# One-core decoder trunk: V projected together with the forget gate, a reworked recurrent stage, other unit orders and buffer counts

## Chip, core and metric

The kernel runs on one core of one Trainium2 chip. The metric is device time in microseconds (us). It is written in a tile framework: the order of TensorE's instructions is the order of the program text (a manual schedule), the other engines' orders are set by the framework's scheduler, and the framework places all semaphores.

## What is computed

A sequence of 256 tokens with 1024 channels passes through two layers. Layer 0 is FFN, RG-LRU recurrent block, FFN; layer 1 is FFN, forgetting attention, FFN. Keys, values and the forget gate's running sum are computed once, between the layers. Every sub-layer has an RMSNorm before and behind it.

```python
def swiglu(x, w_gate, w_up, w_down):
    return (jax.nn.silu(x @ w_gate) * (x @ w_up)) @ w_down        # 1024 -> 2816 -> 1024

def rg_lru(x, ...):                                               # 16 blocks of 84 channels
    r = sigmoid(blockdiag(x, w_a) + b_a); i = sigmoid(blockdiag(x, w_x) + b_x)
    log_a = -8 * r * softplus(-lam); a = exp(log_a)
    u = sqrt(-expm1(2 * log_a)) * (i * x)
    return scan(h = a * h + u)

def recurrent_block(x, ...):
    gate, rec = split(x @ w_in)                                   # 2 x 1344 columns
    return (gelu(gate) * rg_lru(conv4(rec))) @ w_out

kv = hn @ w_kv; log_f = log_sigmoid(hn @ w_f + b_f); c = cumsum(log_f)   # w_f: 1024 x 16
logits = q k^T + c_q - c_k, causal; softmax; @ v; @ w_o           # 16 heads of 64
```

## The kernel before

**Units.** The 256 tokens are two tiles of 128, t = 0 and t = 1. All weights (float32) stream once through SBUF in units of up to 128 x 1024. A unit is loaded into a `raw` buffer (tag `raw`, `RAW` = 3 of them) by SP's DMA queue, and split (`split`, lines 169 to 182) into a high part `whi` (ScalarE, line 178; the first four units on GpSimd, line 176) and the rest `wlo` (VectorE, line 179). There are `WB` = 10 pairs of these. A product is three matmuls in the reduced float32 format, high by high, high by low, low by high (`mm3`, lines 184 to 188; `mm3w`, 190 to 195, with the weights stationary).

**Order.** `items` is the list of units in the order in which they are loaded, each with a `prep` (load and split) and a `work`. `slot(t, i)` runs the matmuls of unit i for tile t and then calls `tick()`, which counts down the deferred functions (`defer(n, fn)` runs fn n ticks later), prepares the next unit if a pace model says that its load has landed (`prepare_next`, which won't prepare unit i before unit i - WB has been used by both tiles), and takes pieces of VectorE and ScalarE work from `queue`. `run` (line 334) lets tile 0 run ahead of tile 1 by `lag` slots: 7 at the start and end of a stage, 4 (`MID`) in between. So each unit stays in its buffers until tile 1 has used it. One slot is six matmuls of 512 columns.

**FFN stage.** `proj_items` makes the units of the gate and up projections (two blocks of 128 rows by 512 columns each), `row_items` those of the projections back to 1024 channels: there a unit is one block of 128 rows, and each tile accumulates in two PSUM banks. With `rows` = 1 a unit's matmuls run as they come; a higher `rows` holds back the last `rows` units of tile 1 so that all their work for the first bank comes before that for the second. `enter` (line 247) closes such a stage: Squares on ScalarE out of both banks (line 208), the norm's factor on GpSimd (lines 201 and 203), the new `h` on VectorE (line 260), and some ticks later the transposes of `h` (line 217, or with `normed`, used for the first FFN alone, line 284 on a normed copy `hn`) and the split into `xhi` and `xlo`.

**Recurrent stage.** Its order is written out in `RG_ORDER` (line 818). Names such as `0g3` are gate units for tile 0, 11 in three column groups (0 to 3, 4 to 7, 8 to 10); `r2` is a pair of units that gives channels tiles 4 and 5 of the recurrent input for all 256 tokens (`add_rec_units`), followed by the convolution in `conv` (ScalarE line 641, VectorE line 647) and its own split into `ch` (line 649) and `cl` (line 652). `gw2` is a unit of its own with the block-diagonal weights of the two gates, loaded by up to eight small DMAs into a zeroed raw buffer (lines 666 to 676), split like others, and multiplied in three matmuls per product with `ch` and `cl`. Behind it follow tanh (694), scaling on VectorE (711), tanh and exp (714, 715), a Newton step (720 to 725), square root (739), products (744, 745) and the scan (749). For every two pairs, `batch` transposes the gate projection (757), takes its gelu (759), multiplies (771) and splits into `yh` (773) and `yl` (778). w_out (11 row units) follows with `run`; `get_yy` forces the queue's work for group 0, 1 or 2 to be issued before row 0, 4 or 8.

**Shared K/V and attention.** V is two `proj_items` of 512 columns, four units each, with the forget gate's 16 columns as a unit of its own between them (lines 926 to 940); `running` (line 915) makes the running sum nine ticks later. The attention stage has its own order in `ATT_ORDER`: `0` and `1` are slots of tile 0 and 1 for the q and output projections, `a0` and `a1` steps of attention for a tile.

PSUM has four banks `mm`, two `gt`, two `tr`.

Of the kernel before, what the change touches and what calls it, by code (L numbers as in the profile page):

```python
# [28 lines left out]
RAW = 3  # L29
WB = 10  # L30
# [14 lines left out]
def trunk_kernel(ctx: ExitStack, tc: tile.TileContext, A: dict, out: bass.AP):  # L45
# [201 lines left out]
    def enter(t, dests, pf, gb, half, last=False, normed=False):  # L247
# [24 lines left out]
        def norm():  # L272
            stat(t)
            hn = []
            for n in range(2):
                hn.append(hpool.tile([P, 512], F32, tag="t1", name=nm("hn"), bufs=2))
                nc.vector.tensor_scalar(hn[n], h[t][:, n * 512:(n + 1) * 512], rs[t][:, 0:1], None, ALU.mult)

            def go():
                tps = []  # L280
                for n in range(2):
                    tp = gtbank()
                    for j in range(4):
                        nc.tensor.transpose(tp[:, j * P:(j + 1) * P], hn[n][:, j * P:(j + 1) * P], ident)
# [110 lines left out]
    def row_items(w, widths, get_x, post, rows=1):  # L395


        acc = {}
        kept = []
        nk = len(widths)  # L400
        r0 = 0
        for k, kp in enumerate(widths):
            def prep(kp=kp, r0=r0):
                return split(load_raw(w[r0:r0 + kp, :], kp, D), kp, D)

            def work(t, u, k=k):
                if k == 0:
                    acc[t] = [mmbank(), mmbank()]
                if t == 1 and k >= nk - rows:
                    kept.append((k, u))  # L410
                    if k < nk - 1:
                        return
                    todo = [(kk, uu, n) for n in range(2) for (kk, uu) in kept]
# [19 lines left out]
    def ffn_items(pool_of, wg, wu, wd, post_g, next_dests, last=False, normed=False):  # L433
# [55 lines left out]
        row_items(wd, [P] * 22, lambda t, k: (hid[t][0][:, k, :], hid[t][1][:, k, :]), post_down, 4 if last else 1)  # L489
# [46 lines left out]
    sp2 = rw.tile([RT, NRT], F32, name="sp2")  # L536

# [7 lines left out]
    def rg_params():  # L545
# [8 lines left out]
        def rest():  # L554
# [3 lines left out]
            nc.vector.tensor_scalar(sp2, sp, 2.0, None, ALU.mult)  # L558
        defer(1, rest)

# [14 lines left out]
    xcs, chs, tt, th, yy = {}, {}, {}, {}, {}  # L575

    def add_gate_unit(g, k0, kn):
# [5 lines left out]
        def work(t, u):  # L583
# [47 lines left out]
    def conv(p, ps):  # L631
        tl, w = tiles_of(p), pw(p)
        m = len(tl)
# [3 lines left out]
        ch = pools["r"].tile([RT, 2, S], F32R, tag="ch", name=nm("ch"), bufs=2)  # L637
        cl = pools["r"].tile([RT, 2, S], F32R, tag="cl", name=nm("cl"), bufs=2)
        xcs[p], chs[p] = xc, (ch, cl)
# [4 lines left out]
        def taps(j, i):  # L644
# [4 lines left out]
            nc.scalar.activation(ch[:w, j, :], xc[:w, j, :], AF.Copy)  # L649

        def low():
            nc.vector.tensor_tensor(cl[:w, :m, :], xc[:w, :m, :], ch[:w, :m, :].bitcast(F32), ALU.subtract)

        first = [(1.25, ("c", p), lambda j=j, i=i: taps(j, i)) for j, i in enumerate(tl)] + [(0.65, ("c", p), low)]
# [3 lines left out]
    def add_gw_unit(p):  # L658
        tl, w = tiles_of(p), pw(p)
        m = len(tl)  # L660
        n = m * RT if m == 2 else BLK

        def prep():
            raw = new_raw()
            v = raw[:w, :2 * m * n]
# [11 lines left out]
            return split(v, w, 2 * m * n)  # L677

        def work(t, u):
# [3 lines left out]
            ch, cl = chs[p]  # L683
# [16 lines left out]
        rg[f"gw{p}"] = len(items)  # L700
        items.append((prep, work))

    def after_gates(p):
# [3 lines left out]
        t_ = tt[p][:w, :m, :] if p in tt else None  # L707
# [11 lines left out]
        def newton():  # L719
            nc.vector.tensor_scalar(z, z, 0.5, 0.5, ALU.mult, ALU.add)  # L720
            nc.vector.scalar_tensor_tensor(b, tt[p][:w, :m, :], 1.0, z, ALU.add, ALU.mult)
# [6 lines left out]
        queue.extend([(1.1 * s, ("n", p), zz), (1.0 * s, ("n", p), newton), (1.0 * s, ("n", p), newton2)])  # L728
# [3 lines left out]
    def batch(g):  # L732

        pairs = [p for p in (2 * g, 2 * g + 1)]

        def roots():
            for p in pairs:
                v = tt[p][:pw(p), :len(tiles_of(p)), :]
                nc.scalar.activation(v, v, AF.Sqrt)

        def u_of(p):
            w, m = pw(p), len(tiles_of(p))
            v = tt[p][:w, :m, :]
# [3 lines left out]
        def scan(p, j):  # L747
            w = pw(p)
            nc.vector.tensor_tensor_scan(tt[p][:w, j, :], th[p][0][:w, j, :], tt[p][:w, j, :], 0.0, ALU.mult, ALU.add)

        def gelu(t):
            tok = toks[(g, t)]
            tp = trbank()
            y = pools["r"].tile([RT, 4, P], F32, tag="y", name=nm("y"), bufs=2)
# [3 lines left out]
            for (a, b, w) in parts_of(g):  # L758
                nc.scalar.activation(y[:w, a:b, :], tp[:w, a * P:b * P].rearrange("p (a b) -> p a b", a=b - a),
                                     AF.Gelu_apprx_tanh)  # L760
            ys[(g, t)] = y

        def product(t):
            y = ys[(g, t)]
            if t not in yy:
                yy[t] = (pools["r"].tile([RT, NRT, P], F32R, name=f"yh{t}"), pools["r"].tile([RT, NRT, P], F32R, name=f"yl{t}"))
            yh, yl = yy[t]
            for jj, p in enumerate(pairs):
                w, m = pw(p), len(tiles_of(p))
                v = y[:w, 2 * jj:2 * jj + m, :]  # L770
                nc.vector.tensor_tensor(v, v, tt[p][:w, :m, t * P:(t + 1) * P], ALU.mult)
            for (a, b, w) in parts_of(g):
                nc.scalar.activation(yh[:w, 4 * g + a:4 * g + b, :], y[:w, a:b, :], AF.Copy)

        def low(t):
            y, (yh, yl) = ys[(g, t)], yy[t]
            for (a, b, w) in parts_of(g):
                nc.vector.tensor_tensor(yl[:w, 4 * g + a:4 * g + b, :], y[:w, a:b, :],
                                        yh[:w, 4 * g + a:4 * g + b, :].bitcast(F32), ALU.subtract)
# [7 lines left out]
        q.insert(2, (0.0, key, lambda: gelu(0)))  # L787
        q.insert(3, (0.0, key, lambda: gelu(1)))
# [5 lines left out]

    ys = {}
# [7 lines left out]
    add_rec_units(0)  # L803
    add_rec_units(1)
    add_gw_unit(0)
    add_rec_units(2)
    add_gw_unit(1)
    add_rec_units(3)
    add_gw_unit(2)
    for k0 in (0, 3, 6):  # L810
        add_gate_unit(2, k0, min(3, 8 - k0))
    add_rec_units(4)
    add_gw_unit(3)
    add_rec_units(5)
    add_gw_unit(4)
    add_gw_unit(5)
# [11 lines left out]
    def get_yy(t, k):  # L828
        flush(("y", k // 4))
        w = width(k)  # L830
        return yy[t][0][:w, k, :], yy[t][1][:w, k, :]
# [60 lines left out]
    def post_v(n):  # L892
        def f(t, ps):
            nc.scalar.activation(kv["v"][t][:, n * 512:(n + 1) * 512], ps, AF.Copy, scale=rs[t][:, 0:1])
        return f

    def post_f(t, ps):
# [8 lines left out]
        def rest():  # L906
# [5 lines left out]
            defer(9, lambda: running(t))  # L912
# [13 lines left out]
    proj_items(A["w_kv"], D, 512, z_x, post_v(0))  # L926

    def prep_f():
        raw = new_raw()
        nc.sync.dma_start(raw[:, :P].rearrange("p (k n) -> p k n", k=8), A["w_fgate"].rearrange("(k p) n -> p k n", p=P))  # L930
        return split(raw[:, :P], P, P)

    def work_f(t, u):
        ps = mmbank()[:, :NH]
        for k in range(8):
            mm3(ps, *z_x(t, k), u.hi[:, k * NH:(k + 1) * NH], u.lo[:, k * NH:(k + 1) * NH], k == 0, k == 7)
        post_f(t, ps)

    items.append((prep_f, work_f))
    proj_items(A["w_kv"], D + 512, 512, z_x, post_v(1))  # L940
# [92 lines left out]
    for n in range(2):  # L1033
# [11 lines left out]
    ATT_ORDER = ("0 0 0 0 0 0 0 0 a0 1 a0 1 1 a0 1 a0 1 a0 1 a0 1 a0 a1 1 a0 a1 "  # L1045
                 "0 a1 0 a1 0 a1 0 a1 0 a1 0 a1 0 a1 0 a1 1 a1 1 a1 1 1 1 1 1 1")
# [29 lines left out]
    run(n_ffn1, lag_in=3)  # L1076
# [3 lines left out]
    for name in RG_ORDER:  # L1080
# [8 lines left out]
        else:  # L1089
            slot(None, rg[name])  # L1090
    state["a"] = state["b"] = n_rg
    run(n_wout)
# [61 lines left out]
```

## Time and profile before

| | us |
|---|---|
| median of 3 runs (lowest, highest) | 1058.16 (1056.62, 1058.39) |
| the profiled execution | 1056.71 |
| its span, first to last instruction | 1055.0 |
| TensorE busy, weight loads, VectorE, ScalarE | 1019.9, 843.2, 624.0, 539.3 |
| mean granted TensorE clock | 0.982 |
| VectorE's largest group, line 179 (`wlo`), 338 instructions | 408.0 |
| ScalarE's largest group, line 178 (`whi`), 332 instructions | 348.6 |

A page has the busy time of each engine, the span in 40 slices, DMA queues, the chain that ended last and the costliest groups. Matmuls overlap, so their busy time says where TensorE is idle and not how fast it goes; that is read from the starts of successive matmuls. A wait is given as engine, line, what it waited for, then total us, times, and the longest. Windows are stretches of the span with each engine's busy time and the share of the full clock that was granted. Stages by time: first FFN to about 211, recurrent stage to 346, second FFN to 534, K/V and third FFN to about 785, attention to 860, last FFN to the end.

### The profile page before, as it was taken

The numbers are of one execution on the slowest core, as the hardware profiler recorded it, in microseconds if no ns is written. First come the engines' busy times: TensorE is split into PE (matmuls) and PEld (weight loads), VectorE is DVE, ScalarE is ACT, GpSimd is POOL, SyncE is SP. The second block draws the span as 40 slices with busy tenths as digits, with TensorE's granted clock in tenths as the row PEclk, the third lists the DMA queues.
The fourth block names the chain that finished last, engine by engine and source line by source line (L and its number), as shares of the span: only waits on it lengthen the run. The fifth ranks groups of instructions, "written<-read, shape, count | busy, mean of one in ns | idle before, by whom it ended". The sixth has DMA issues, their size and how long they took to land.

```text
span 1055.0 us, 13090 instructions
## 1 busy us (share of the span) xinstructions
PE 1019.9 (97%) x4870; PEld 843.2 (80%) x4870; DVE 624.0 (59%) x771; ACT 539.3 (51%) x739; POOL 48.7 (5%) x109
## 2 busy tenths in 40 slices
PE   7999999989978999999999999999999999999997
PEld 4778888779966888888878888888888888888885
DVE  4666554548997755554486455555476475555542
ACT  3555543538886644443355444444357574454431
POOL 4200000010001100000010000000010010000000
PEclk9999999989988999999999999999999999999999
DMA  5776655536245676655446666655563156766541
GB/s 185 236 221 196 182 188 189 160 88 161 70 158 161 203 213 192 183 181 195 142 160 181 178 180 180 195 182 184 190 203 113 49 161 178 200 180 189 190 140 40
DMA packets 90742, 178.86 MB, mean 170 GB/s; under 512 B 11694, under 2 KB 28150, under 8 KB 90678
## 3 DMA queue, kind: packets, MB, share of 16 engines
q1 hardware_dynamic: 90006, 177.94, 55.9%
q8 instruction: 38, 0.62, 0.2%
q14 instruction: 26, 0.21, 0.1%
q0 software_dynamic: 640, 0.07, 0.1%
q10 hardware_dynamic: 32, 0.01, 0.0%
HBM read 176.95 MB, written 1.05 MB: 169 GB/s over the span
## 4 chain that ended last, share of the span: by engine, by line
PE 83%; DVE 6%; ACT 4%; DMA 4%; issue 2%; POOL 1%; DVEq 0%; SPq 0%; POOLq 0%; ACTq 0%
PE mm L186 25%; PE mm L188 25%; PE mm L187 25%; DVE wlo L179 3%; PE tr L462 2%; DMA raw<-in_ffn_w_gate_dram 2%; ACT whi L178 1%; PE mm L997 1%; PE gt L970 1%; ACT junk L208 1%; DMA raw<-in_ffn_w_up_dram 1%; PE gt L217 1%; PE tr L883 1%; PE mm L195 1%; PE mm L193 1%
## 5 line engine op out<-in xcount | busy, mean ns | idle before, releaser
L179 DVE TENSOR_TENSOR wlo<-raw,whi 128x1024 fp32r<-128x1024 f32 (+3 forms) x338 | 408.0, 1210 | 312.8 <-ACT whi L178 307.6
L178 ACT ACTIVATE whi<-raw 128x1024 fp32r<-128x1024 f32 (+2 forms) x332 | 348.6, 1052 | 359.9 <-PE mm L188 290.9
L186 PE MATMUL mm<-whi,xhi 128*128 128x512 f32 (+2 forms) x784 | 312.3, 398 | 5.3 <-ACT xhi L229 3.3
L187 PE MATMUL mm<-wlo,xhi 128*128 128x512 f32 (+2 forms) x784 | 306.4, 391 | 1.5 <-DVE wlo L179 1.5
L188 PE MATMUL mm<-whi,xlo 128*128 128x512 f32 (+2 forms) x784 | 306.5, 391 | 0.0
L186 PEld LDWEIGHTS mm<-whi,xhi 128*128 128x128 f32 x784 | 148.6, 189 | 35.2 <-POOL whi L176 3.4
L188 PEld LDWEIGHTS mm<-whi,xlo 128*128 128x128 f32 x784 | 148.3, 189 | 31.7 <-DVE xlo L232 0.6
L187 PEld LDWEIGHTS mm<-wlo,xhi 128*128 128x128 f32 x784 | 148.7, 190 | 30.5 <-DVE wlo L179 2.1
L186 PE MATMUL mm<-whi,hhi 128*128 128x512 f32 x352 | 139.5, 396 | 0.0
L188 PE MATMUL mm<-whi,hlo 128*128 128x512 f32 x352 | 139.0, 395 | 0.0
L187 PE MATMUL mm<-wlo,hhi 128*128 128x512 f32 x352 | 138.7, 394 | 0.0
L188 PEld LDWEIGHTS mm<-whi,hlo 128*128 128x128 f32 x352 | 66.1, 188 | 15.4
L187 PEld LDWEIGHTS mm<-wlo,hhi 128*128 128x128 f32 x352 | 66.1, 188 | 15.3
L186 PEld LDWEIGHTS mm<-whi,hhi 128*128 128x128 f32 x352 | 66.1, 188 | 15.1
L456 DVE SCALAR_TENSOR_TENSOR prod<-mm,rstd,sil 128x512 f32<-128x512 f32 (+1 forms) x48 | 33.9, 705 | 37.8 <-PE mm L188 34.0
L447 ACT ACTIVATE sil<-mm,rstd 128x512 f32<-128x512 f32 (+1 forms) x48 | 31.3, 651 | 44.9 <-PE mm L188 44.9
L201 POOL TENSOR_SCALAR nv<-ss 128x1 f32<-128x1 f32 x24 | 9.4, 391 | 759.6 <-ACT junk L208 759.6
L256 DVE TENSOR_TENSOR t<-mm,gb 128x512 f32<-128x512 f32 x24 | 16.3, 688 | 31.1 <-ACT junk L208 30.8
L466 ACT ACTIVATE hhi<-tr 128x512 fp32r<-128x512 f32 (+1 forms) x48 | 26.6, 553 | 14.6 <-PE tr L462 14.5
L467 DVE TENSOR_TENSOR hlo<-tr,hhi 128x512 fp32r<-128x512 f32 (+1 forms) x48 | 30.5, 642 | 3.4 <-ACT hhi L466 1.5
L208 ACT ACTIVATE junk<-mm 128x512 bf16<-128x512 f32 x24 | 14.2, 592 | 33.2 <-PE mm L188 32.8
L186 PE MATMUL mm<-whi,zhi 128*128 128x512 f32 (+1 forms) x80 | 31.0, 387 | 0.0
(178 smaller groups left out, 950.7 us busy)
## 6 DMA issues: line engine op xcount, KB each, us to landing
raw<-in_ffn_w_down_dram SPq DMA_DIRECT2D x88, 512.0 KB
raw<-in_ffn_w_up_dram SPq DMA_DIRECT2D x80, 512.0 KB
raw<-in_ffn_w_gate_dram SPq DMA_DIRECT2D x78, 512.0 KB
raw<-in_rg_w_in_dram SPq DMA_DIRECT2D x20, 504.0 KB
raw<-in_w_kv_dram SPq DMA_DIRECT2D x16, 512.0 KB
raw<-in_ffn_w_gate_dram SPq DMA_DIRECT2D x20, 256.0 KB
raw<-in_rg_w_out_dram SPq DMA_DIRECT2D x10, 504.0 KB
raw<-in_ffn_w_up_dram SPq DMA_DIRECT2D x16, 256.0 KB
```

The lines of the kernel that those rows point to most:

```text
L178: nc.scalar.activation(hi[:parts, c:c + m], rawv[:, c:c + m], AF.Copy)
L179: nc.vector.tensor_tensor(lo[:parts, c:c + m], rawv[:, c:c + m], hi[:parts, c:c + m].bitcast(F32), ALU.subtract)
L186: nc.tensor.matmul(ps, xh, wh, start=first, stop=False)
L187: nc.tensor.matmul(ps, xh, wl, start=False, stop=False)
L188: nc.tensor.matmul(ps, xl, wh, start=False, stop=last)
L208: nc.scalar.activation(junk[:, :src.shape[1]], src, AF.Square, scale=f, accum_out=acc)
L256: nc.vector.tensor_tensor(t1[n], pf[n], gb[:, n * 512:(n + 1) * 512], ALU.mult)
L447: nc.scalar.activation(s[:, :nn], ps, AF.Silu, scale=rs[t][:, 0:1])
L456: nc.vector.scalar_tensor_tensor(pr[:, :nn], ps, rs[t][:, 0:1], s, ALU.mult, ALU.mult)
L462: nc.tensor.transpose(tp[:, j * P:(j + 1) * P], pr[:, j * P:(j + 1) * P], ident)
L466: nc.scalar.activation(hv, tp[:, :nn], AF.Copy)
L467: nc.vector.tensor_tensor(lv, tp[:, :nn], hv.bitcast(F32), ALU.subtract)
```

## The change

- **Buffers.** `RAW` 3 to 5, `WB` 10 to 9.
- **Row units.** `row_items` holds back the last two units by default, for tile 0 as well (tile 0 never more than two); the last FFN keeps four for tile 1.
- **First FFN's end.** `norm` sums the squares of `h` in two halves and is called at once instead of a tick later; its transposes come five ticks on, not two after the one; tile 0 may be 8 slots ahead at the end (`lag_out=8`).
- **Gate projection.** Gelu is taken straight from the PSUM bank in token layout, for (group 0, tile 1) and (group 2, tile 0) only when the next finished one is due, so those banks are held; `batch` transposes the result after the scans, and multiplies out of PSUM.
- **Gates.** No `ch` and `cl`; the block-diagonal weights aren't split and aren't units any more. They are loaded during the first FFN (ahead of its units 20, 26, ... 50) into six buffers of their own and multiplied in plain float32, one matmul instruction per product, with `xc`. `yh` and `yl` later use the same six buffers. `tensor_work`, which feeds the pace model, isn't called for these.
- **After the gates.** Scaling goes into the tanh's and exp's scale and bias (22 ScalarE calls on 256 columns for 12 on up to 512 and 11 VectorE ones); `tt` is one tile for each group of two pairs, so that the square root is one call (two in the last group).
- **Orders.** A new `RG_ORDER`; w_out in a written order `OUT_ORDER`: eight slots of tile 0, four of tile 1, three of 0, seven of 1. A new `ATT_ORDER`.
- **V.** Three column groups of 344, 340 and 340; the first has the 16 forget-gate columns in the same units. Four units each, with `running` fifteen ticks later.

```diff
-RAW = 3
-WB = 10
+RAW = 5
+WB = 9
...
         def norm():
-            stat(t)
+            ss = new_ss()
+            for n in range(2):
+                square_sum(h[t][:, n * 512:(n + 1) * 512], ss[:, n:n + 1])
+            rs[t] = rstd_of(ss, 2)
...
-            defer(2, go)
+            defer(5, go)
...
-            defer(1, norm)
+            norm()
...
-                if t == 1 and k >= nk - rows:
-                    kept.append((k, u))
+                m = rows if t == 1 else min(rows, 2)
+                if k >= nk - m:
+                    kept[t].append((k, u))
...
-                tok = pools["r"].tile([P, 4 * RT], F32, tag="tok", name=nm("tok"), bufs=4)
-                nc.scalar.activation(tok[:, :nn], ps, AF.Copy)
-                toks[(g, t)] = tok
+                if (g, t) not in ((0, 1), (2, 0)):
+                    for gg, tt_ in {(1, 1): [(0, 1)], (2, 1): [(2, 0)]}.get((g, t), []) + [(g, t)]:
+                        n = GCOLS[gg][1]
+                        tok = toks[(gg, tt_)] = pools["r"].tile([P, 4 * RT], F32, tag="tok", name=nm("tok"), bufs=4)
+                        nc.scalar.activation(tok[:, :n], gacc[(gg, tt_)][:, :n], AF.Gelu_apprx_tanh)
...
-            nc.scalar.activation(ch[:w, j, :], xc[:w, j, :], AF.Copy)
-
-        def low():
-            nc.vector.tensor_tensor(cl[:w, :m, :], xc[:w, :m, :], ch[:w, :m, :].bitcast(F32), ALU.subtract)
...
-            raw = new_raw()
-            v = raw[:w, :2 * m * n]
+            v = box["w"] = rw.tile([P, 1024], F32, tag="gy", name=nm("gw"), bufs=6)[:w, :2 * m * n]
...
-            return split(v, w, 2 * m * n)
...
-                        mm3w(ps[:w, j * S:(j + 1) * S], u.hi[:, o:o + w], u.lo[:, o:o + w], ch[:w, k, :], cl[:w, k, :],
-                             k == 0, k == m - 1)
+                        nc.tensor.matmul(ps[:w, j * S:(j + 1) * S], wv[:, o:o + w], xc[:w, k, :],
+                                         start=k == 0, stop=k == m - 1)
...
+        ahead(20 + 6 * p, prep)
+        gw[p] = work
...
-            for j, i in enumerate(tl):
-                nc.vector.tensor_scalar(th[p][0][:w, j, :], th[p][0][:w, j, :], sp2[:w, i:i + 1], sp2[:w, i:i + 1],
-                                        ALU.mult, ALU.add)
-            tt[p] = pools["r"].tile([RT, 2, S], F32, tag="tt", name=nm("tt"), bufs=6)
-            nc.scalar.activation(tt[p][:w, :m, :], z, AF.Tanh)
-            nc.scalar.activation(z, z, AF.Exp, scale=-2.0)
+            for (dst, f, c) in ((t_, AF.Tanh, sp2), (th[p][0], AF.Exp, sp4)):
+                for j, i in enumerate(tl):
+                    nc.scalar.activation(dst[:w, j, :], th[p][0][:w, j, :], f, bias=c[:w, i:i + 1], scale=c[:w, i:i + 1])
...
-        q.insert(2, (0.0, key, lambda: gelu(0)))
-        q.insert(3, (0.0, key, lambda: gelu(1)))
+        q.append((0.0, key, lambda: (gate_T(0), gate_T(1))))
...
-    RG_ORDER = ("0g0 0g1 0g2 0g3 0g4 0g5 0g6 0g7 r0 1g0 1g1 1g2 1g3 r1 gw0 1g4 1g5 r2 gw1 1g6 1g7 r3 gw2 "
-                "0g8 0g9 0g10 r4 gw3 1g8 r5 gw4 1g9 1g10 gw5").split()
+    RG_ORDER = ("0g0 0g1 0g2 0g3 0g4 0g5 0g6 0g7 1g0 1g1 r0 1g2 r1 gw0 1g3 1g4 r2 gw1 1g5 1g6 r3 gw2 1g7 "
+                "0g8 0g9 0g10 r4 gw3 r5 1g8 1g9 gw4 1g10 gw5").split()
+    OUT_ORDER = [0] * 8 + [1] * 4 + [0] * 3 + [1] * 7
...
-            defer(9, lambda: running(t))
+            defer(15, lambda: running(t))
...
+    VCOLS = [(0, 344), (344, 340), (684, 340)]
...
-    ATT_ORDER = ("0 0 0 0 0 0 0 0 a0 1 a0 1 1 a0 1 a0 1 a0 1 a0 1 a0 a1 1 a0 a1 "
-                 "0 a1 0 a1 0 a1 0 a1 0 a1 0 a1 0 a1 0 a1 1 a1 1 a1 1 1 1 1 1 1")
+    ATT_ORDER = ("0 0 0 0 0 0 0 0 a0 1 a0 1 1 1 a0 1 a0 1 a0 1 a0 a1 1 a0 "
+                 "0 a1 a0 a1 0 a1 0 a1 0 a1 0 a1 0 a1 0 a1 0 a1 1 a1 1 a1 1 1 1 1 1 1")
...
-    run(n_ffn1, lag_in=3)
+    run(n_ffn1, lag_in=3, lag_out=8)
```

More of the change, by code (lines that the diff above doesn't have):

```diff
@@ L536, in trunk_kernel @@
     sp2 = rw.tile([RT, NRT], F32, name="sp2")
+    sp4 = rw.tile([RT, NRT], F32, name="sp4")
     def rg_params_load():
@@ L574, in trunk_kernel @@
     toks = {}
[L575 removed]
+    xcs, tt, th, yy = {}, {}, {}, {}
     def add_gate_unit(g, k0, kn):
@@ L757, in gelu, with product, low @@
                 nc.tensor.transpose(tp[:w, j * P:(j + 1) * P], tok[:, j * RT:j * RT + w], ident)
-            for (a, b, w) in parts_of(g):
[L759 to L771, printed above, removed]
-            for (a, b, w) in parts_of(g):
[L773 to L779, printed above, removed]
+        def product(t):
+            y = ys[t] = pools["r"].tile([RT, 4, P], F32, tag="y", name=nm("y"), bufs=2)
+            if t == 0:
+                yy[g] = [rw.tile([P, 1024], F32R, tag="gy", name=nm("y"), bufs=6).rearrange("p (t a b) -> p t a b", t=2, a=4)
+                         for _ in range(2)]
+            for (a, b, w) in parts_of(g):
+                tp = tps[t][:w, a * P:b * P].rearrange("p (a b) -> p a b", a=b - a)
+                nc.vector.tensor_tensor(y[:w, a:b, :], tp, tt[g][:w, a:b, t * P:(t + 1) * P], ALU.mult)
+                nc.scalar.activation(yy[g][0][:w, t, a:b, :], y[:w, a:b, :], AF.Copy)
+        def low(t):
+            yh, yl = yy[g]
+            for (a, b, w) in parts_of(g):
+                nc.vector.tensor_tensor(yl[:w, t, a:b, :], ys[t][:w, a:b, :], yh[:w, t, a:b, :].bitcast(F32), ALU.subtract)
         key = ("y", g)
@@ L802, in trunk_kernel @@
             add_gate_unit(g, k0, 2)
[L803 to L809, printed above, removed]
+    for p in range(4):
+        add_rec_units(p)
     for k0 in (0, 3, 6):
@@ L1089, in trunk_kernel @@
         else:
-            slot(None, rg[name])
-    state["a"] = state["b"] = n_rg
-    run(n_wout)
+            gw[int(name[2:])]()
+    nxt = [n_rg, n_rg]
+    for t in OUT_ORDER:
+        slot(t, nxt[t])
+        nxt[t] += 1
+    state["a"], state["b"] = nxt
     rcm.__exit__(None, None, None)
```

101 lines of the change are left out of this document (56 added, 45 removed).

## Prediction

> **What bounds the kernel now.** I read the page's busy shares and its 40 slices first, then the windows of 20 us, then TensorE's waits, then the timeline inside the windows that stood out. Columns of a window row: length, then PE, PEld, DVE, ACT, POOL busy (instructions), granted clock, DMA share, GB/s.
>
> ```profile
> span 1055.0 us, 13090 instructions
> PE 1019.9 (97%) x4870; PEld 843.2 (80%) x4870; DVE 624.0 (59%) x771; ACT 539.3 (51%) x739; POOL 48.7 (5%) x109
> PEclk9999999989988999999999999999999999999999
> ```
> ```profile
> 200.00:220.00 20.00, 15.18 (x69) 11.83 (x67) 16.75 (x22) 12.08 (x18) 5.02 (x8) 0.96 0.64 180
> ...
> 280.00:300.00 20.00, 15.48 (x109) 15.02 (x109) 17.91 (x35) 17.84 (x29) 0.00 (x0) 0.91 0.44 137
> 300.00:320.00 20.00, 17.22 (x75) 13.08 (x74) 19.90 (x37) 18.36 (x26) 0.00 (x0) 0.91 0.44 142
> 320.00:340.00 20.00, 15.59 (x58) 11.72 (x57) 14.63 (x24) 11.13 (x21) 0.87 (x2) 0.83 0.55 163
> ```
> ```profile
> PE mm L186 <- ACT yh L773: 6.8, 2, 4.4
> PE gt L284 <- DVE hn L277: 4.9, 2, 3.6
> PE gt L194 <- DVE cl L652: 4.4, 1, 4.4
> ```
>
> TensorE sets the time: it works 97% of the span, and in the FFN stages it never waits. So time comes or goes in two ways only: TensorE gets more or less to do, or one of its few waits changes. The waits sit in four places: the start (0 to 60), the step from the first FFN to the recurrent stage (204 to 225), the tail of the recurrent stage (280 to 331), and short ones at 540 and 801. In the tail VectorE is busy 52.4 of 60 us: there it is the bound, and TensorE waits for `cl` and twice for `yh`. Each long wait also costs afterwards: the granted clock goes to half for 3.4 or 6.8 us.
>
> Busy time hides what one matmul costs, since matmuls overlap; start-to-start times from the timeline tell it. First the gates, then the forget gate and what follows it; last, from the chain of waits, four records of an attention product with 256 columns in plain float32.
>
> ```profile
> 248.16 0.28 PE L193 MATMUL gt<-ch,whi 126*126 126x256 f32 x1
> 248.28 0.28 PE L194 MATMUL gt<-cl,whi 126*126 126x256 f32 x1
> ```
> ```profile
> 542.73 0.26 PE L186 MATMUL mm<-whi,zhi 128*128 128x16 f32 x1
> 542.84 0.26 PE L187 MATMUL mm<-wlo,zhi 128*128 128x16 f32 x1
> ...
> 547.30 0.63 PE L187 MATMUL mm<-wlo,zhi 128*128 128x512 f32 x1
> 547.72 0.63 PE L188 MATMUL mm<-whi,zlo 128*128 128x512 f32 x1
> ```
> ```profile
> 835.95 0.86 PE gt L970 x4
> ```
>
> A 256-column piece takes 0.12 us, a 16-column one 0.11, a 512-column one 0.227 (0.43 at half clock, as here), a 336-column one 0.153.
>
> **The parts.** All against the profiled execution, 1056.7 us (span 1055.0 and 1.7 around it).
>
> *V and forget gate: -4.3.* The 48 matmuls of 16 columns go: 48 x 0.111 = 5.3. V had 96 of 512: 96 x 0.2265 = 21.7. It gets 48 of 360 and 96 of 340 columns; between the rows for 336 and 512 a column costs 0.42 ns, so 0.163 and 0.155: 7.8 + 14.9 = 22.7. Sum 22.7 - 27.0. Twelve splits in place of nine, but smaller, lie beside TensorE; 1344-byte packets take 58 ns against 84 for 2048, so the loads cost the DMA engines about 0.6 us more in a stage where they are busy 0.45 to 0.65.
>
> *The clock after the forget gate: -2.9.* At 546.1 and 563.2, just behind each of the two stretches of 24 tiny matmuls, the clock is halved for 3.4 us; some eight matmuls there take 0.43 instead of 0.23: 1.4 + 1.5. No gap over 0.1 us stands between the tiny ones, so I put the drop down to how little each of them does. Ends: -2.9 and 0.
> The Trainium skill ("TensorE: Matmul & The Clock Gate", "Why this matters for your kernels") asks only that no gap between bursts exceeds about 3 us, and by that rule these drops wouldn't come from matmuls without gaps and needn't go with them. By it this term is 0 and the time 2.9 higher, as in rival 1.
>
> *Gates in plain float32: +3.0.* Now 42 products x 3 pieces x 0.1195 = 15.1. For the new form the nearest row is L970, and its count matters: 32 attention products (16 heads, two tiles) stand as 64 records, so a float32 product runs as two, each 0.86/4 = 0.215 for 256 columns. 42 x 0.43 = 18.1. One instruction in place of three is therefore slower on TensorE. Ends: -5.0, if a record takes the 0.12 of the present pieces, and +11.8, if its weight load isn't hidden (0.105, the spacing of the 64-column products of L997).
>
> *Tail of the recurrent stage: -10.* Idle in 280 to 340 is 4.5 + 2.8 + 4.4 = 11.7; half clock (293.6 to 297.0, 310.6 to 314.0, 326.1 to 331.1) adds about 6: 17.7 lost. VectorE loses `cl` (3.8), line 711 (4.6) and six `wlo` of gate weights (5 x 1.12 + 0.25 = 5.9): 14.3. ScalarE loses `ch` (4.6), six `whi` (5.5), the gelus on transposed tiles (3.2; the copies to `tok` turn into gelus at the same price), and gets 22 x 0.42 = 9.2 for 7.2: 11.3 less; it also loads tables 14 times here, 1.28 each, which I leave. From 240 to 330 VectorE had some 81 us of work and gets 67; TensorE's own work there is 90 - 17.7 + 3 = 75. So VectorE stops being the longer of the two. The `cl` wait (4.4) goes. What is late next is the last group's `yh`: from the last gates (301.6) to 326.1 it took 24.5 us, while TensorE had nine row slots of 1.4. Now it has twelve (16.8), but that chain goes through some 10 us in series (tanh, exp, a square-root table, scan, product) behind about 8 of the group before and the splits of w_out, with the gate's transposes now last instead of early. I keep 8 of 17.7. Ends: 0 and -17.7, and above nothing by rival 3.
>
> *Step into the recurrent stage: -5.5.* Lost now: 1.2 + 3.6 idle, and 2.4 by half clock (until 225.3): 7.2. The transposes come one slot (1.38) later. For tile 1 the chain from the last matmul (210.9) to `hn` takes 9.1; 1.4 of it is a `whi` waiting 0.65 for its DMA ahead of the second Square (211.7 to 212.6), which two more raw buffers spare; two half Squares and a first bank that ends one row earlier save about 0.6 each. Some 6.9 remain against five slots of 1.38 = 6.9. Ends -1.4 and -7.2.
>
> *Start: -2.* At 26.1 TensorE waits 1.8 + 0.8 for unit 4's split, and half clock takes 1.6 more. Five raw buffers let loads and splits be placed earlier, though ScalarE stands behind a Silu there. Ends 0 and -4.1.
>
> *Step into the shared K/V: +0.5.* TensorE waits 1.35 at 538.6 for `h`. The three slots ahead of these transposes shrink from 1.37 to 0.98: +1.2; the row hold gives 0.7 back. Ends -0.7 and +3 (a half clock).
>
> *Attention list: -1.* One more matmul slot before the second step covers most of the 1.3 wait for `qT`. Ends -1.4 and +2.
>
> *At nothing.* 42 loads of gate weights (0.4 us of SP's queue each) move into the first FFN; SP stands waiting for a free raw buffer there anyway (lines 163 and 166: 731 us in all), and the weights lie split 14 us before use, so 3.4 us per batch are covered. Without that cover each batch would cost up to 3.4. Nine split buffers: outside the recurrent stage and the start, the smallest lead of a split over its first use is 6.9 us, and one buffer less takes a pair of slots, 2.75, off it. Held-back rows elsewhere: nothing waits there.
>
> Sum: -4.3 - 2.9 + 3.0 - 10 - 5.5 - 2 + 0.5 - 1 = -22.2: 1034.5 in the profiled execution. The median of the runs, 1058.2, lies 1.4 above that execution, so **1036**.
>
> **Rivals.** (1) *The clock falls anyway* behind the step at 540 or for another cause: 1036 + 2.9 = 1039. For: 1.35 us of idle stand before the first drop. Against: none stands before the second. Chance 0.10.
> (2) *The chain to the last `yh` stays as long.* For: 14 table loads, and the gate's transposes moved behind the scans; against: 14 us less on the engine that was full. The tail gives nothing: 1036 + 10 = 1046. Chance 0.20.
> (3) *Slower: the ninth buffer.* Eight gate units stay held until tile 1 uses them, so the second halves of r0 to r3 and unit 0g8 may be split only after a slot that comes just before. If the split gets the buffer which that very slot frees, TensorE waits: 1.05 + 1.2 + 0.3 = 2.55, less 1.43 of cover (12 x 0.119), 1.1 each at four places and 2.4 at 0g8: 6.8, and a half clock behind each, 5 x 1.7 = 8.5. With the tail's gain lost too: 1046 + 15.3 = 1061. It decides when a split starts less than 2.55 us before use; if an older free buffer is taken, as there are, it costs nothing. Chance 0.08.
>
> **Numbers.** My forecast, own range 1028 to 1043: 0.58. Between (2) and (3), within 0.2% of 1058.2 (2.1 us, about what a measurement tells from no change): 0.04. Faster 0.88, same 0.04, slower 0.08. The range 1026 to 1049 takes in (1), (2) and the ends of the larger terms added as independent; about 0.2 stays out.
>
> **What would show it.** Right: no 16-column matmul, and full clock between 540 and 580; 84 gate records about 0.215 apart; no wait for `cl`, VectorE below 18 of 20 us before w_out, one short `yh` wait left; under 1.5 us of `hn` wait. Wrong: gate records at 0.12 (then 8 us better), waits of r1 to r3 for `whi` or `wlo`, a late `yh` as long as before, or new waits for raw loads in the FFNs.

## The result, and the profile after

The changed kernel takes 1024.78 us, median of four runs (1024.45 to 1024.98); the kernel before, beside it, 1057.62 (1056.62 to 1058.39). The ratio is 0.969, 95% interval 0.9673 to 0.9707. The forecast was 1036 with 1026 to 1049: right side, but the gain was 33 and not 22, and the time lies 1.2 below the range.

The page of the changed kernel, with the lines that answer to those of before (TensorE is idle 19 of 1023 us, and the dips of the clock have gone but for one at the start; a last one, behind the last matmul, both kernels have):

```profile
span 1022.7 us, 12958 instructions
PE 1003.8 (98%) x4828; PEld 834.2 (82%) x4828; DVE 609.2 (60%) x748; ACT 533.1 (52%) x732; POOL 52.9 (5%) x109
PEclk9899999999999999999999999999999999999999
```

Its windows at the step into the recurrent stage and in the tail, columns as before:

```profile
200.00:220.00 20.00, 19.67 (x94) 15.65 (x93) 17.49 (x24) 13.47 (x23) 3.00 (x6) 1.00 0.77 233
...
280.00:300.00 20.00, 20.00 (x107) 17.55 (x106) 18.46 (x34) 19.85 (x31) 0.00 (x0) 1.00 0.21 66
300.00:320.00 20.00, 19.24 (x92) 15.69 (x91) 19.50 (x33) 13.44 (x22) 3.02 (x7) 1.00 0.63 192
320.00:340.00 20.00, 19.50 (x92) 15.82 (x91) 13.70 (x17) 11.09 (x17) 6.84 (x8) 1.00 0.61 192
```

TensorE had 15.2 to 17.2 busy at a clock of 0.83 to 0.96 in these rows; now it has 19.2 to 20.0 at full clock. The rows don't hold the same work, since the changed kernel begins w_out 12 us earlier, at 289.5. In 280 to 300, up to the gates' end, VectorE and ScalarE are still at 18.5 and 19.9 of 20. The waits of TensorE (total, times, longest; in this kernel the tiles of both parts, `yh` and `yl`, are named `y`, the high one written in L773 and the low one in L778):

```profile
PE mm L186 <- POOL whi L176: 2.6, 2, 2.4
PE mm L186 <- ACT whi L178: 1.8, 1, 1.8
...
PE gt L217 <- DVE h L260: 1.7, 2, 1.2
...
PE mm L188 <- DVE y L778: 0.8, 1, 0.8
...
PE gt L287 <- DVE hn L280: 0.3, 1, 0.3
```

The 6.8 for `yh` and 4.4 for `cl` are gone, but for 0.8 for the low part of `y`, and the 4.9 for `hn` is 0.3. What is left is the start (the first two rows among others) and 1.2 for `h` at the step to K/V. Length of the stages, between the starts of the same matmuls in both kernels (w_out is counted to its last product, K/V to the first matmul behind its last):

| us | before | after | change |
|---|---|---|---|
| start and first FFN | 210.8 | 208.0 | -2.7 |
| recurrent stage up to w_out | 90.8 | 81.5 | -9.3 |
| w_out | 44.0 | 32.2 | -11.8 |
| second FFN and step to K/V | 188.6 | 189.5 | +0.9 |
| K/V | 63.1 | 55.1 | -8.0 |
| third FFN, attention, last FFN | 457.7 | 456.4 | -1.3 |

For the tail I use one more measure, the **lost time**: by how much the time from one matmul's start to the next exceeds the usual one for that instruction. The usual one is the median of the run for that instruction and shape, and shorter steps count against longer ones. It counts idle time and half clock alike. In the tail, here from 240 us to the last matmul of w_out, it was 18.6 us before (the prediction's 17.7, and small pieces) and is 1.2 after; in the step into the stage (200 to 240) 7.2 and 0.8.

### The profile page after: what moved, and what is told of

Same layout as the page of the kernel before. It is cut to its first block, busy times and chain, and to the rows that moved or that the text cites. A ratio compares the mean times of both kernels' runs of the same rounds, so it can differ in the third digit from the quotient of the medians.

```text
span 1022.7 us, 12958 instructions
## 1 busy us (share of the span) xinstructions
PE 1003.8 (98%) x4828; PEld 834.2 (82%) x4828; DVE 609.2 (60%) x748; ACT 533.1 (52%) x732; POOL 52.9 (5%) x109
## 4 chain that ended last, share of the span: by engine, by line
PE 88%; DVE 4%; ACT 3%; issue 2%; POOL 1%; DMA 1%; SPq 0%; DVEq 0%; POOLq 0%; ACTq 0%
PE mm L188 26%; PE mm L186 26%; PE mm L187 26%; PE tr L466 2%; DVE wlo L179 1%; PE gt L694 1%; PE mm L193 1%; PE mm L194 1%; PE mm L195 1%; PE gt L973 1%; PE mm L1000 1%; DMA raw<-in_ffn_w_gate_dram 1%; ACT junk L208 1%; PE tr L874 1%; PE gt L217 1%
## 5 line engine op out<-in xcount | busy, mean ns | idle before, releaser
L179 DVE TENSOR_TENSOR wlo<-raw,whi 128x1024 fp32r<-128x1024 f32 (+5 forms) x335 | 400.3, 1201 | 286.0 <-ACT whi L178 279.6
L178 ACT ACTIVATE whi<-raw 128x1024 fp32r<-128x1024 f32 (+4 forms) x329 | 342.1, 1045 | 322.4 <-PE mm L188 261.8
L187 PEld LDWEIGHTS mm<-wlo,hhi 128*128 128x128 f32 x352 | 66.2, 188 | 15.1
L256 DVE TENSOR_TENSOR t<-mm,gb 128x512 f32<-128x512 f32 x24 | 16.2, 688 | 29.8 <-ACT junk L208 29.7
L471 DVE TENSOR_TENSOR hlo<-tr,hhi 128x512 fp32r<-128x512 f32 (+1 forms) x48 | 30.5, 643 | 2.8 <-ACT hhi L470 1.5
L186 PE MATMUL mm<-whi,zhi 128*128 128x340 f32 (+2 forms) x80 | 28.5, 356 | 0.0
```

The costliest lines, as they stand in the source:

```text
L178: nc.scalar.activation(hi[:parts, c:c + m], rawv[:, c:c + m], AF.Copy)
L179: nc.vector.tensor_tensor(lo[:parts, c:c + m], rawv[:, c:c + m], hi[:parts, c:c + m].bitcast(F32), ALU.subtract)
L186: nc.tensor.matmul(ps, xh, wh, start=first, stop=False)
L187: nc.tensor.matmul(ps, xh, wl, start=False, stop=False)
L256: nc.vector.tensor_tensor(t1[n], pf[n], gb[:, n * 512:(n + 1) * 512], ALU.mult)
L471: nc.vector.tensor_tensor(lv, tp[:, :nn], hv.bitcast(F32), ALU.subtract)
```

## Experiments

Each was timed beside the kernel before on its own chip, where that took 1055.2 to 1057.7. So ratios are compared, and the profiled spans by stage. "After" is 0.969 and 1022.7. A span is one execution of four, so where it and the ratio differ, the ratio counts. The first row of stages is 206.9 to 209.0 in the changed kernel and four versions of it whose edits don't touch the start: about a microsecond there means nothing.

**V and forget gate alone** (all else as before).

```diff
+    VCOLS = [(0, 344), (344, 340), (684, 340)]
...
+                if extra:
+                    nc.sync.dma_start(v[:, :, n:], A["w_fgate"][rows, :].rearrange("(k p) n -> p k n", p=P))
```

> The kernel before with V's three column groups and the forget gate inside the first of them, and nothing else. By my terms: -4.3 for the columns, -2.9 for the clock that no longer falls behind the tiny matmuls, +1.2 because the three slots ahead of the transposes of h get shorter: -6.0, about 1052 where the kernel before has 1058. If the clock falls for another cause (the wait for h at 538), the -2.9 stays out: about 1055, and the records from 540 to 570 still show half clock.

Measured 0.9918 (0.9893 to 0.9943), so 6.0 to 11.3 less; span 1048.9, -6.1, in the slowest of the four. The K/V stage shrank by 7.0, and its clock is whole. Two rows of before, then of this version:

```profile
540.00:560.00 20.00, 19.96 (x100) 16.77 (x101) 14.33 (x35) 10.20 (x15) 1.73 (x3) 0.91 0.47 157
560.00:580.00 20.00, 20.00 (x97) 16.62 (x97) 11.94 (x28) 9.17 (x12) 1.45 (x5) 0.91 0.63 185
```
```profile
540.00:560.00 20.00, 20.00 (x125) 19.67 (x124) 18.21 (x55) 12.02 (x22) 1.11 (x4) 1.00 0.66 200
560.00:580.00 20.00, 18.47 (x91) 15.23 (x90) 11.58 (x13) 10.48 (x12) 0.45 (x3) 1.00 0.78 229
```

The changed kernel still waits 1.2 for `h` there, with its clock whole, so the half clock came with the 24 tiny matmuls and not with that wait. The 1.5 that TensorE is idle in the second row is a wait for `htok` that the slower stage had covered.

**The gates' matmuls twice.** Each product of the gates is issued two times in a row, with the result unchanged.

```diff
-                    for k in range(m):
+                    for k in list(range(m)) * 2:
```

> The changed kernel with every gate matmul issued twice into the same bank (the sum is started again, so the result stays). TensorE gets 18.1 us more at 0.43 a product. If TensorE bounds the whole recurrent stage now: +17 to +19. If ScalarE (over 19 of 20 us busy from 240 to 300) or the chain to the last yh is close behind, the stage had no room and the sum is the same, but the wait of 0.8 at w_out goes: +17. Under +14 would mean that TensorE waits somewhere that the start-to-start times don't show.

Measured 0.9865 (0.9851 to 0.988), span +16.2; the stage up to w_out is 18.1 longer: 42 products at 0.43. TensorE's own work sets the time of this stage now, and the float32 product costs what the prediction took. In the timeline of the changed kernel a gate of two tiles is

```profile
283.61 3.62 PE L694 MATMUL gt<-xc,gw 126*126 126x256 f32 x16
```

16 records for 8 products; the median from one record's start to the next is 0.216.

**w_out in the order of run.**

```diff
-    for t in OUT_ORDER:
-        slot(t, nxt[t])
...
+    run(n_wout)
```

> The changed kernel with w_out's slots in the order of the kernel before (seven of tile 0, then alternating: row 8 of tile 0 comes after nine slots, not twelve). Theory A (the order made the room): three slots of 1.4 less room for a chain that takes 18 us now, so a wait of 4 to 6 us at row 8, perhaps a half clock behind it: +4 to +8, about 1030. Theory B (the engines' relief alone ended the waits): under +1, 1025.

Measured 0.9721 (0.97 to 0.9742), span +2.7, w_out +3.6. The wait is for the high part now and 1.8 longer, and a half clock behind it costs another 1.8:

```profile
PE mm L186 <- ACT y L773: 2.6, 1, 2.6
```

**VectorE's 14 us put back** as work that nobody reads: `cl` and the scaling at their old places, `wlo` of the gate weights ahead of the gate's products.

```diff
+            nc.vector.tensor_tensor(pools["r"].tile([RT, 2, S], F32R, tag="cl", name=nm("cl"), bufs=1)[:w, :len(tl), :],
+                                    xc[:w, :len(tl), :], xc[:w, :len(tl), :], ALU.subtract)
...
+            nc.vector.tensor_tensor(sp_[:w, :2 * m * n], wv, wv, ALU.subtract)
...
+                nc.vector.tensor_scalar(sc[:w, j, :], th[p][0][:w, j, :], sp2[:w, i:i + 1], sp2[:w, i:i + 1],
+                                        ALU.mult, ALU.add)
```

> The changed kernel with VectorE's removed work put back as work that nobody reads: one 512-column subtraction for each pair (as cl), the scaling of line 711, and one 1008-column subtraction for each gate weight; 14 us in the recurrent stage. Theory B (VectorE's relief ended the waits): they come back, +6 to +15, 1031 to 1040, with waits for yl or yh at w_out. Theory A (the orders): under +2.

Measured 0.9728 (0.9707 to 0.9749), span +5.2, of it 3.6 in the stage up to w_out, 0.4 in w_out and 0.9 at the start, which the edit doesn't touch. That is less than the theory that VectorE's relief ended the waits had asked for, and more than the other had. The largest new wait is ahead of the last gate:

```profile
PE gt L700 <- issue: 1.6, 1, 1.6
```

The view names no releaser, but in the timeline it ends 0.1 us after the tanh with which ScalarE empties the previous gate's PSUM bank, and that tanh stood behind a table load. The runs below with ScalarE's work or three raw buffers back have the same wait (1.5 and 1.6), and the one with three parts back has 3.4.

**ScalarE's 13 us put back** as unread copies of the convolution's result, the gate weights and the transposed gates. The copies took 14.8, while the change had taken 6.2 off ScalarE in all (539.3 to 533.1), so ScalarE is busy 543.5 here, more than before. And they don't all stand at the old places: the copy of the transposed gates comes directly ahead of the one that makes the high part of `y`, where the old gelu stood ahead of the scans.

```diff
+            nc.scalar.activation(pools["r"].tile([P, 512], F32R, tag="sa", name=nm("ca"), bufs=1)[:w, :S], xc[:w, j, :], AF.Copy)
...
+                nc.scalar.activation(sa[:w, :m * n], wv[:, half * m * n:(half + 1) * m * n], AF.Copy)
...
+                nc.scalar.activation(cg[:w, a:b, :], tp, AF.Copy)
```

> The kernel after with the ScalarE work that the change removed put back as unread copies at the old places: 11 copies of the convolution's result, the six gate weights' copies (1008 columns, as two halves), a copy of each transposed gate. By the rows of before that is 4.6 + 5.5 + 3.2, 13.3 us more on ScalarE; VectorE's work stays out. Theory A (with VectorE relieved, ScalarE is what the tail now leans on: it is busy 19.1 to 19.9 of each 20 us from 240 to 300): 8 to 13 us later, 1033 to 1038, more than VectorE's own work cost (4.1). Theory B (its busy time there is mostly queueing behind TensorE and VectorE, which the next slots cover): under 3 us, 1025 to 1028.

Measured 0.9802 (0.9786 to 0.9818), span +11.2, all of it in the stage and w_out. The waits for `y` are back:

```profile
PE mm L186 <- ACT y L779: 4.5, 1, 4.5
...
PE mm L188 <- DVE y L784: 2.2, 1, 2.2
```

From the end of the last gate product to the end of the last high part of `y` it takes 29.0 us here, 18.3 in the changed kernel, 25.5 before and 17.6 with VectorE's work put back. In the changed order, then, ScalarE has little room to spare and VectorE more; the 11 us are the price of this load at these places, and above what ScalarE's relief brought.

**Three and four parts undone at once:** the raw and split buffers as before, w_out by `run`, VectorE's work; and ScalarE's as well.

```diff
-RAW = 5
-WB = 9
+RAW = 3
+WB = 10
```

> The kernel after with three parts undone at once: three raw and ten split buffers, VectorE's 14 us of work put back as unread work in the recurrent stage, w_out in the order of run. Undone one at a time they cost 7.0, 4.1 and 3.3 us by the times, and 3.1, 4.0 and 3.6 of that in the recurrent stage and w_out. Theory A (each part stands for itself): the sum, 14.4, so 1039, with about 10 to 11 of it in the recurrent stage and w_out. Theory B (the parts hide one another: with one undone, the others still give the cover): more than the sum, 1043 to 1048, with 14 to 18 lost in the recurrent stage and w_out, yh waits of 4 us or more and half clocks behind them.

> The kernel after with all four undone: raw and split buffers, w_out's order, VectorE's 14 us and ScalarE's 13 us. Left of the change in this stage are the unit order, the plain float32 gates and the gate transposes behind the scans. Theory A (the tail's gain of 17 is the engines' relief together with w_out's order): the stage and w_out lose at least the 17 again, 1045 to 1055 with the 6 or 7 of the raw buffers. Theory B (the unit order, which spreads the gates over the second tile's gate slots, holds most of it): the loss stays at 8 to 12 in the stage, 1036 to 1042.

Measured 0.9826 (0.9806 to 0.9847) with three, span +11.6, of it 9.0 in the stage and w_out. By the ratios that is 14.4, about the sum of the single ones (3.3, 4.0 and 7.4). The chain from the last gate product to the last high part stays at 18.3, so none of these three had made it short. With four 0.9879 (0.9857 to 0.9902), span +16.9, of it 15.2 there and 14.0 lost in the tail (20 by the ratios, as the profiled execution was the fastest of four). ScalarE's work adds only 6.2 in this stage to what the three cost, though it cost 11.0 alone: in part they cost the same time. Since that work is more than before had, what is left for the unit order, the plain float32 gates and the transposes behind the scans isn't shown, and none of them was undone alone.

**Which engine bounded the tail of before?** Three edits of the kernel before. They change the stage's result: in the first, exp, square root and gelu are tanh, so that ScalarE loads 15 tables fewer, 1.28 us each; in the second `cl`, `wlo` of the gate weights and the scaling are left out, their places in the matmuls taken by the high parts, and a constant bias stands ahead of tanh and exp; the third is both, with a scale of 0.1 in the tanh that stands for exp.

```diff
-            nc.scalar.activation(z, z, AF.Exp, scale=-2.0)
+            nc.scalar.activation(z, z, AF.Tanh, scale=-2.0)
...
-                nc.scalar.activation(v, v, AF.Sqrt)
+                nc.scalar.activation(v, v, AF.Tanh)
```
```diff
-            ch, cl = chs[p]
+            ch = cl = chs[p][0]
...
-            return split(v, w, 2 * m * n)
+            u = Unit()
...
+            u.hi = u.lo = hi[:w, :2 * m * n]
+            return u
```

> The kernel before with exp, square root and gelu of the recurrent stage all computed as tanh, so that the stage's result differs but ScalarE needs one activation table there: about 15 table loads of 1.28, 19 us, leave ScalarE; VectorE and TensorE do what they did. Theory A (ScalarE's queue sets the tail of before, and VectorE's waits are its echo): at least 8 of the 17.7 us lost in the tail go, 1040 to 1048. Theory B (VectorE is the bound of the tail, as the forecast had it): under 4 go, since VectorE's work is unchanged: 1052 to 1056.

> The kernel before without 14.3 us of VectorE's work in the recurrent stage: no cl and no wlo of the gate weights (the high parts stand in for them in the same matmuls), no scaling ahead of tanh and exp (a constant bias stands in). The stage's result differs; TensorE and ScalarE do what they did. Theory A (ScalarE sets the tail): the wait for cl goes, but the yh waits stay, 2 to 6 us less: 1050 to 1054. Theory B (VectorE is the bound): about 10 of the 17.7 go as the forecast had it, 1044 to 1047.

> The kernel before with both: no table loads within the recurrent stage and VectorE without its 14.3 us; the result differs. Either theory: most of the tail's 17.7 goes, 13 or more, 1040 to 1044. If less goes than in the better of the two single ones plus 3, the order of the units (gates late, w_out by run) holds the rest of the loss.

| | ratio (95%) | lost in the tail | last gate product to last `yh` |
|---|---|---|---|
| before | 1 | 18.6 | 25.5 |
| ScalarE lighter by 19 | 0.9981 (0.9968 to 0.9994) | 17.8 | 27.8 |
| VectorE lighter by 14 | 0.9951 (0.9936 to 0.9966) | 11.6 | 26.7 |
| both | 0.9885 (0.9869 to 0.9902) | 5.1 | 17.7 |

Each theory passes one of the first two runs and falls in the other: neither engine was the bound alone. With ScalarE light, TensorE waits as long for `yh`, and VectorE is full:

```profile
PE mm L186 <- ACT yh L773: 7.2, 2, 5.3
...
PE gt L194 <- DVE cl L652: 2.6, 1, 2.6
```
```profile
300.00:320.00 20.00, 13.92 (x54) 10.46 (x53) 19.50 (x38) 10.47 (x21) 0.00 (x0) 0.83 0.29 94
```

With VectorE light (line numbers are three higher in this kernel's helpers) `cl` and `yh` are no longer waited for, but a weight's high part (5.9 in the tail; the 1.8 at the start before has too), since ScalarE's queue is late:

```profile
PE mm L189 <- ACT whi L181: 7.7, 2, 5.9
```
```profile
300.00:320.00 20.00, 13.42 (x46) 9.96 (x44) 18.54 (x34) 18.00 (x28) 0.00 (x0) 0.74 0.40 118
```

Only with both is the chain short and 13.5 of the 18.6 gone; by the times the two singles give 2 and 5 us and the pair 12. The 19 us are three times what the change took off ScalarE, so this shows how the two engines act together and not what the change's own relief is worth.

```profile
300.00:320.00 20.00, 17.66 (x78) 13.71 (x77) 18.09 (x33) 10.18 (x18) 0.00 (x0) 1.00 0.56 171
```

**Buffers alone**, the same two lines as above in the changed kernel.

> The changed kernel with three raw and ten split buffers, as before. If five raw buffers are worth something where stages meet and at the start: +2 to +6, with waits for splits at 20 to 30 us and at the step into the recurrent stage. If they are only spare: within 1. If nine split buffers cost something (my rival 3), ten make it faster by 1 to 5.

Measured 0.976 (0.9735 to 0.9784), span +6.0: the start and first FFN +1.6, the recurrent stage +3.1, the K/V stage and the step to it +1.5. Of the 3.1, 1.1 is a longer wait for `hn` and 1.6 the wait ahead of the last gate. The nine split buffers cost nothing that shows: no unit of r0 to r3 and not 0g8 is waited for in the changed kernel.

**The old step into the recurrent stage:** norm in one Square, its transposes and the lag as before; the held-back row stays.

```diff
-            defer(5, go)
+            defer(2, go)
...
-            norm()
+            defer(1, norm)
```

> The changed kernel with the old step into the recurrent stage: one Square over all of h, norm called a tick later, transposes three ticks on, tile 0 seven slots ahead at most. My term said -5.5 for this, of which the later transposes are 1.4 a tile and the shorter chain the rest. If the reworked step is what saves it: +4 to +6 and a wait of 3 to 4 us for hn, half clock behind it. If the five raw buffers saved most of it (the Square no longer waits behind a split that waits for its load): +1 to +3, with a wait of 1.5 to 2.5.

Measured 0.9728 (0.9713 to 0.9742), span +3.0, so under half of the 6.4 that the step gained. The wait of before is back at two thirds of its size, with no half clock behind it:

```profile
PE gt L284 <- DVE hn L277: 3.1, 2, 1.8
```

**A better start, and a better step to K/V.** The start still loses 7 us between 20 and 32, as the first units are split late. Two calls of `prepare_next(True)` are put ahead of the two tiles' statistics and behind them; then the second tile's transposes behind a step come four ticks on, not three.

```diff
     to_x(tps, main_dest(0, 1))
+    prepare_next(True)
     stat(0)
     stat(1)
+    prepare_next(True)
```
```diff
-            defer(3, inputs)
+            defer(4 if t == 1 else 3, inputs)
```

> The changed kernel with units 3 and 4 prepared earlier in the first 20 us: unit 3 ahead of the two statistics, unit 4 right behind them. In the changed kernel TensorE loses 7 us from 19.8 to 31.4, waiting for the splits of units 3 (GpSimd, behind the norm's factors) and 4 (ScalarE, behind the first Silu), and to half clock behind that. If these positions in the queues are the cause: -4 to -7, about 1019. If the loads are late anyway: within 1, or slower, since ScalarE and GpSimd then stand at a load with the statistics behind them.

> The version with two units prepared early at the start (1018.7) and the second tile's transposes behind each step one slot later (four slots, not three). Theory A (the 1.4 lost at 508 is a fixed chain to h, which one V slot of 0.98 covers in most part): 1.0 to 1.4 less, 1017.5. Theory B (xhi and xlo of that tile become late instead, or a step that had no wait gets one): 1018.7 or up to 1 more.

Measured 1018.73, ratio 0.9649 (0.9631 to 0.9667), span -5.8 with the first, and 1015.98, **0.9616** (0.9598 to 0.9635), span 1013.9 with both. This beats both kernels. The window at the start, of the changed kernel and then of the version with both:

```profile
20.00:40.00 20.00, 16.52 (x59) 12.49 (x59) 11.08 (x10) 10.01 (x11) 14.69 (x27) 0.83 0.58 188
```
```profile
20.00:40.00 20.00, 20.00 (x92) 16.42 (x90) 15.09 (x14) 12.44 (x14) 14.54 (x27) 1.00 0.86 282
```

Of the 3.0 between the two versions' spans, 1.1 came at the start, which the second edit doesn't touch, and 1.9 about the step to K/V.

## Where the prediction was right, and where it failed

| term | forecast | measured |
|---|---|---|
| V and forget gate | -4.3 | -4.2 (48 x 0.164 and 96 x 0.1555 for 27.0) |
| clock after the forget gate | -2.9 | -2.8 (7.0 in the stage, alone) |
| gates in float32 | +3.0 | +3.0 (42 x 0.43 for 15.1) |
| tail of the recurrent stage | -10 | -17.4 (lost time 18.6 to 1.2) |
| step into the recurrent stage | -5.5 | -6.4 (lost time 7.2 to 0.8) |
| start | -2 | -0.1 (lost time up to 60 us: 12.0 to 11.9) |
| rest of the first FFN | 0 | -1.2 (the rest of the first row of stages, without 1.4 of the step) |
| step to K/V | +0.5 | +0.9 with the second FFN |
| attention list | -1 | -0.5 (-2.4, then +1.9) |
| w_out's matmuls, last FFN | 0 | -1.0, -0.8 |
| sum | -22.2 | -30.5, of -32.3 in the span |

**What held.** The prices taken from start-to-start times came out within 0.1 us. Gate records stand 0.216 apart and not 0.12, so one instruction for three was dearer, as a row of the attention stage had said. Against drops of the clock in mid-kernel the Trainium skill ("TensorE: Matmul & The Clock Gate", "Why this matters for your kernels") asks for no idle gap above about 3 us; taken as the only cause, that would have left the drops at 546 and 563 where they were. Without the tiny matmuls they are gone, and here the measurement decides. All three rivals fell: that of the clock, of the ninth split buffer, and of a chain to `yh` that stays as long. One sign stayed out: VectorE, which was to be below 18 of 20 us before w_out, is at 18.7 and 18.5 from 260 to 300.

**What failed: "I keep 8 of 17.7".** Twelve row slots, 16.8 us, were rightly counted as cover, so keeping 8 meant a chain from the last gates to the last `yh` of about 25, hardly shorter than the one of before (24.5 there, 25.5 as counted in the table above). It measures 18.3, and 1.2 is lost, 0.8 of it a wait. That is 7.4 of the 10.1 by which the spans and the forecast differ. The pieces which the step itself named, 10 in series behind 8 of the group before, come to 18; the 8 us kept had no sum behind them. The step also took VectorE for the bound, compared its load alone with TensorE's, and listed ScalarE's 11.3 us of relief without giving it a price. Even that size was off: the 22 calls that take scale and bias from a tile last 0.60 each on 256 columns, as long as the old ones on 512, and not 0.42. Before, then after:

```profile
L715 ACT ACTIVATE th<-th 126x512 f32<-126x512 f32 (+1 forms) x6 | 3.6, 593 | 0.0
L714 ACT ACTIVATE tt<-th 126x512 f32<-126x512 f32 (+1 forms) x6 | 3.6, 592 | 0.0
```
```profile
L720 ACT ACTIVATE th<-th,sp 126x256 f32<-126x256 f32 (+1 forms) x11 | 6.5, 596 | 0.1
L720 ACT ACTIVATE tt<-th,sp 126x256 f32<-126x256 f32 (+1 forms) x11 | 6.2, 598 | 0.0
```

So they cost 13.1 (22 x 0.597) for 7.1, and with one more table load ScalarE lost 6.2. In the kernel before the runs show two full queues that hand the chain back and forth: lightening either leaves the other in the way (17.8 and 11.6 still lost), lightening both frees 13.5 of 18.6. Put back one by one in the changed kernel, ScalarE's work (more than was taken away) costs 11.0, VectorE's 4.0, w_out's order 3.6 and the buffers 3.2 of the stage and w_out; with all four it is 15.2 and not their 21.8, so here the losses overlap. What made the chain itself 7 us shorter stays open between ScalarE's relief, the unit order, the plain float32 gates and the gelu that is taken earlier; with VectorE's work, w_out's order and the buffers as before it stays short.

**Smaller misses.** At the step into the stage, 6.9 of work against 6.9 of cover came out with 0.3 of wait and no half clock, within the ends that the term had. The reworked step holds only 3.0 of the 6.4; with three raw buffers 1.1 of it goes too. The start gave nothing: TensorE waits 1.8 and 0.8 for unit 4's split as before, since five raw buffers don't help while that split waits in its queue; moving the call does (-5.8). Most of the first FFN's 1.2 is a wait of 0.7 for `prod` at 63 us, which is gone; the prediction had it that TensorE never waits in the FFN stages. The -2.4 before the output projection and the +1.9 behind it were not separated by a run, and 1.8 of the span's gain is in no row.

## What to carry to other kernels

Where two engines pass a chain back and forth and both are near full, price the relief on both together: here lightening both gave 12 us where the two alone gave 2 and 5, and an experiment that lightens one shows little. When work is put back in an experiment, compare the engine's total with that of before: 13 us by the prediction's rows were 14.8, for a relief of 6.2. The engine named as the releaser of a wait is only the last in that chain. Price matmuls from start to start, and look for stretches of very small ones: they cost their own 0.11 us each and here, mostly, the clock behind them too.

## What was not expected of the hardware

Row matmuls of 512 columns start 0.235 us apart on `yh` in w_out before, 0.227 on `y` after (132 of them, so 1 us); those of the FFN's hidden rows 0.233 in both. The stationary tile and its pool differ; which matters wasn't tried. The order isn't it: with w_out by `run` it is 0.227 too.

And 24 matmuls of 16 columns in a row, with no gap above 0.1 us, can halve the granted clock for 3.4 us, as long as many a wait did. Of the eight such stretches in the traces of before and of its three edits, seven are followed by a half clock. The falls of the clock have a grid: in each trace every one comes a whole number of 3.41 us after the first. The seven stretches lay with 2.1 us or more in one period of it, and the fall came at that period's end. The eighth (541.2 to 543.8, with ScalarE lighter) lay across a boundary, with 0.8 us in one period and 1.8 in the next, and no fall came. So whether such a stretch costs a half clock depends also on where it falls.
